# Slot tables and one-hot blocks of a two-layer mixture-of-experts kernel: from fp32r to bf16 in parts

## Chip, cores and metric

The kernel runs on one core of a Trainium2 chip. The metric is the time of one execution on the device in microseconds (us); of several executions the median is taken. Three runs of the kernel before gave 2065.88, 2066.47 and 2069.43 us.

## What is computed

Two transformer layers over 512 tokens of width 1024. Each has a dense part (attention and a second mixer, with their projections) and then a layer of experts. For the experts a router picks, for each token, 2 of 32 experts in the first layer and 8 of 64 in the second, each with a weight; every expert is a gated feed-forward network with 256 hidden columns, and a token's result is the weighted sum over its experts.

```python
# first layer                                  # second layer
g_w, g_idx = lax.top_k(g_prob, 1)              e_w: top 8 of sigmoid(router) + bias,
e_w, e_idx = lax.top_k(softmax(e_sel), 2)      normalised, times 2.5
weights = g_w * e_w / sum(e_w)
ys = ragged_dot(silu(ragged_dot(xs, w_gate, sizes)) * ragged_dot(xs, w_up, sizes), w_down, sizes)
out = einsum('nkd,nk->nd', ys, weights)
```

All weights are f32. Those of the experts are 3 MB each, so 96 MB in the first layer and 192 MB in the second, and every expert is read once.

## The kernel before

The kernel is one long program in which a planner lays out the instructions of all engines. Work is written as tasks (Python generators); `Flow` wakes the task that is due, and a clock of its own (`Clock.note`) reckons what each instruction will take on its engine. Nearly every instruction goes through the wrapper at line 131, so all rows of the profile bear L131 and are told apart by their tiles. The order that comes out is fixed: each engine works off its own queue in it.

**Layout of the program.** Dense part of the first layer, then its expert loop (`Experts.run`, some 400 to 690 us), a dense part of the second layer, its expert loop (some 1380 to 2040 us), and the last norm. While a dense part still runs, SP already loads the first experts' weights into free buffers. The weights are loaded in chunks of 512 KB, six an expert (four for gate and up, two for down), into tiles named `w` and `wx`; SP issues the load for a chunk when a buffer is given back. Experts are visited in an order made from their counts, and each place in it has a planned number of slots (`PLAN1`, `PLAN2`: blocks of 16 to 128 slots).

**Routing.** `Route.tile` finds for each of the four tiles of 128 tokens which experts are chosen (`sel`) and with which weight. `Route.finish` (from line 2000) puts them in the order of the experts by matmuls with a permutation, writes that order to `self.order` (SP reads it for the addresses of the weights), counts slots by matmuls with a triangle and with ones in bf16 (`slots`, `counts`), and fills the table `R`: for each expert and each of the four token tiles, 128 rows of four fp32r numbers, which are the slot number (0 where the expert is not chosen), the token number + 1, and the weight in a rounded part and the rest. The token numbers are put there early by `Route.table` (line 1903) on GpSimd. The split of the weight is ACT (rounded copy), then DVE (the rest); DVE then writes the slot numbers.

**A block of slots.** `Experts.block` (line 2224) turns a part of the table into the list of tokens of one block: DVE compares the slot numbers with a row of numbers (`ios`, bf16) and gives a one-hot block `oh` (128 tokens x C slots, for four token tiles); PE multiplies it by `R` in four matmuls into four columns; DVE makes the index (`iv`, out of range where the slot is empty) and the weight from these in four small operations; GpSimd gathers the rows of the tokens (`xg`) with an indirect DMA. Blocks are made up to three ahead of their use (`AHEAD`). The first three are made in `begin` (their one-hot blocks are `h` tiles). In `run` the first loads into the extra buffers `wx` wait for the first gather (`b.gate`).

**An expert.** PE transposes the gathered rows (`xT`), multiplies by gate and up, ACT and DVE make the activation (`a`, times the weight), PE transposes it (`aT`) and multiplies by down, ACT and DVE bring the result out (`y`), and GpSimd adds it to the sum in memory with an indirect DMA (`acc_d`). `Experts.rest` (line 2447) is a loop for experts that hold more tokens than planned; the number of its turns is known at run time.

Of the kernel before, what the change touches and what calls it, by code (L numbers as in the profile page):

```python
# [10 lines left out]
F32 = mybir.dt.float32  # L11
F32R = mybir.dt.float32r
BF16 = mybir.dt.bfloat16
I32 = mybir.dt.int32
U32 = mybir.dt.uint32
AF = mybir.ActivationFunctionType
ALU = mybir.AluOpType
AX = mybir.AxisListType
# [3 lines left out]
P = 128  # L22
# [3 lines left out]
NT = T // P  # L26
# [1836 lines left out]
class Route:  # L1863
# [38 lines left out]

    def table(self, pool):
        b, nc = self.b, self.b.nc
        self.R = pool.tile([P, self.E, NT, 4], F32R, name="R")
        tok = b.small(NT)
        nc.gpsimd.iota(tok, pattern=[[P, NT]], base=1, channel_multiplier=1, allow_small_or_imprecise_dtypes=True)
        nc.gpsimd.tensor_copy(self.R[:, :, :, 1], tok.unsqueeze(1).to_broadcast([P, self.E, NT]))

    def tile(self, t, h, keep=None):  # L1910

# [88 lines left out]
    def finish(self):  # L2000

        b, nc, E, F = self.b, self.b.nc, self.E, self.first
        while len(self.sels) < NT or not self.chosen:
            yield 1
        yield W
        rank = yield from self.ranks(NT, True)
        oh = b.h()[:E, :E]
        nc.vector.tensor_scalar(out=oh, in0=self.rank[:E], scalar1=rank, scalar2=None, op0=ALU.is_equal)
        while None in self.parts:
            yield 1  # L2010
        yield W
        po, ps = yield from b.banks(2)
        nc.tensor.matmul(po[:, 0:E], self.iop[:E].to_broadcast([E, P]), oh, start=True, stop=True)
        ps = ps[:, : NT * 2 * E].rearrange("p (t c e) -> p t c e", t=NT, c=2)
        for c in range(2):
            for t in range(NT):
                nc.tensor.matmul(ps[:, t, c], self.parts[t][:, c], oh, start=True, stop=True)
        yield W
        sels = b.h(BF16)[:, : NT * E].rearrange("p (t e) -> p t e", t=NT)
        nc.vector.tensor_copy(sels, ps[:, :, 0])  # L2020
        nc.vector.tensor_copy(self.order[:, F:], po[:, F:E])
        self.known(E)
        yield W
        for t in range(NT):
            self.slots(po[:, (t + 1) * E : (t + 2) * E], [sels[:, u] for u in range(NT)], t)
        et = lambda c: self.R[:, :, :, c].rearrange("p e t -> p t e")
        b.split(ps[:, :, 1], et(2), et(3))
        yield W
        nc.vector.scalar_tensor_tensor(out=et(0), in0=po[:, E : (NT + 1) * E].rearrange("p (t e) -> p t e", t=NT), scalar=1.0, in1=sels, op0=ALU.add, op1=ALU.mult)
        self.counts(po[:, (NT + 1) * E : (NT + 2) * E], [sels[:, t] for t in range(NT)])  # L2030
        nc.scalar.activation(self.orow, po[:, 0:E], AF.Copy)
        yield W
        nc.scalar.activation(self.cnt, po[:, (NT + 1) * E : (NT + 2) * E], AF.Copy)
        b.back(2)
# [45 lines left out]
class Router1:  # L2080


    n = 36
# [50 lines left out]
class Router2:  # L2134


    n = 64
# [25 lines left out]
class Experts:  # L2163
# [57 lines left out]
        for g in self.xgs:  # L2221
            self.b.nc.gpsimd.memset(g, 0.0)

    def block(self, R, n, C, oh):


        b, nc = self.b, self.b.nc
        x = SimpleNamespace(n=self.n, C=C, xg=self.xgs.popleft() if self.xgs else self.ring[self.n % 4])
        self.n += 1
        oh = oh("oh", F32R)[:, : NT * C].rearrange("p (t c) -> p t c", t=NT)  # L2230
        nc.vector.tensor_tensor(out=oh, in0=b.ios[:, n : n + C].unsqueeze(1).to_broadcast([P, NT, C]),
                                in1=R[:, :, 0].bitcast(F32).unsqueeze(2).to_broadcast([P, NT, C]), op=ALU.is_equal)
        yield
        pt, = yield from b.banks(1)
        for t in range(NT):
            nc.tensor.matmul(pt[:C, 0:4], oh[:, t], R[:, t], start=(t == 0), stop=(t == NT - 1))
        yield
        v = b.const.tile([P, 4], F32, name="iv", tag="iv", bufs=8)[:C]
        it = v[:, 2:3].bitcast(I32)
        nc.vector.scalar_tensor_tensor(out=v[:, 1:2], in0=pt[:C, 1:2], scalar=0.0, in1=b.beyond[:C], op0=ALU.is_equal, op1=ALU.mult)  # L2240
        nc.vector.scalar_tensor_tensor(out=it, in0=pt[:C, 1:2], scalar=-1.0, in1=v[:, 1:2], op0=ALU.add, op1=ALU.add)
        nc.vector.tensor_copy(v[:, 1:2], pt[:C, 3:4])
        nc.vector.tensor_tensor(out=v[:, 0:1], in0=pt[:C, 2:3], in1=v[:, 1:2], op=ALU.add)
        b.back(1)
        x.idx, x.w = it, v[:, 0:1]
        x.dma = nc.gpsimd.indirect_dma_start(out=x.xg[:C], out_offset=None, in_=self.h2_d, in_offset=bass.IndirectOffsetOnAxis(ap=it, axis=0),
                                             bounds_check=T - 1, oob_is_err=False)
        return x
# [126 lines left out]

    def fetched(self, i, n, C):
        r = self.route
        self.xs[i].append((yield from self.block(r.R[:, i], sum(r.plan[i][:n]), C, self.oh)))

    def run(self, nx, after={}):  # L2380
        b, nc, E, r = self.b, self.b.nc, self.E, self.route
# [65 lines left out]
    def rest(self, K):  # L2447

        b, nc, E = self.b, self.b.nc, self.E
# [5 lines left out]
        wx = lambda name, dt=F32: x_.pool.tile([P, 1024], dt, name=name, tag=x_.tag, bufs=x_.cap)  # L2455
        n = nc.values_load(ovr[0:1, 3:4], min_val=0, max_val=E + T * K // P)  # L2456
        with b.tc.If(n > 0):
            with b.tc.For_i(0, n, 1) as i:
                ev, place = (nc.values_load(ovr[0:1, bass.ds(i * 4 + k, 1)], min_val=0, max_val=E - 1) for k in (0, 2))
                R, sv = self.mp.tile([P, NT, 4], F32R, name="rR"), self.mp.tile([P, 1], F32, name="rs")  # L2460
                nc.sync.dma_start(R.bitcast(F32), self.route.R.bitcast(F32)[:, bass.ds(place, 1)].rearrange("p o t c -> p (o t) c"))
                nc.sync.dma_start(sv, self.route.lsv[bass.ds(i, 1)].rearrange("o p -> p o"))
                nc.vector.tensor_scalar(out=R[:, :, 0], in0=R[:, :, 0].bitcast(F32), scalar1=sv, scalar2=None, op0=ALU.subtract)
                gu, dn = self.weights(ev)
                ws = []

                def load():
                    if len(ws) < 6:
                        ws.append(wx("w"))
                        nc.sync.dma_start(ws[-1], self.part(gu, dn, len(ws) - 1))  # L2470

                load()
                load()
                self.n = 0
                x = b.at_once(self.block(R, 0, P, wx))
                self.xT(x)

                for c in range(4):
                    self.gu(x, c, ws[c])
                    load()  # L2480
                self.act(x)
                self.aT(x)
                for c in range(2):
                    self.dn(x, c, ws[4 + c])
                    load()
                self.add(x)
# [117 lines left out]
```

## Time and profile before

| | |
|---|---|
| median of three runs | 2066.47 us (2065.88 to 2069.43) |
| the profiled execution | 2071.1 us, of which the span of the profile is 2069.3 us |
| mean granted clock of TensorE | 0.932 |
| PE busy (matmuls) | 1805.0 us, 87% |
| DVE busy | 1098.4 us, 53% |
| ACT busy | 641.6 us, 31% |
| GpSimd (POOL) busy | 321.4 us, 16% |
| moved by DMA | 549.72 MB, mean 266 GB/s |

PE is TensorE's matmuls, PEld its weight loads, DVE VectorE, ACT ScalarE, POOL GpSimd and SP the queue that issues most DMAs (the letter q behind an engine means its queue). A row of a timeline gives start and length in us, engine, line, operation, tiles out<-in, shape and count; in brackets stands the idle time of the engine before it and what ended that. A row of waits gives who waited for whom, the total in us, how often, and the longest. The shares of the whole span mix stages with different limits, so the rows further on are of single stretches.

### The profile page before, as it was taken

How to read it: one execution, taken by the hardware profiler on the slowest of the kernel's cores; microseconds unless marked ns; L12 is line 12 of the kernel's file. 1: busy time of each engine (PE TensorE's matmuls, PEld its weight loads, DVE VectorE, ACT ScalarE, POOL GpSimd, SP SyncE). 2: the span in 40 equal slices, each digit the busy share in tenths (PEclk: the TensorE clock that was granted, in tenths of full speed). 3: DMA queues.
4: the chain of work that ended last, by engine and by line, in shares of the span. 5: the costliest groups of instructions: out<-in, count | busy, mean ns of one | idle time of the engine just before them, and what ended most of it. 6: DMA issues, size and time to landing. Idle time of an engine off the chain costs nothing. (4 is left out here: it accounts for less than half of the span.)

```text
span 2069.3 us, 36349 instructions
## 1 busy us (share of the span) xinstructions
PE 1805.0 (87%) x13053; PEld 1162.7 (56%) x13053; DVE 1098.4 (53%) x3182; ACT 641.6 (31%) x1443; POOL 321.4 (16%) x359
## 2 busy tenths in 40 slices
PE   4999978498877579889999998889999999999993
PEld 3777764354344467667767677664544445455551
DVE  5554763543333365456655565765554455555553
ACT  3522452222222242356653223421211112211121
POOL 1000000123222000000000311022322222222221
PEclk9999988599976699999999999999999999999997
DMA  9745424499999956775423556569999999999996
GB/s 340 270 161 195 154 79 186 159 352 371 376 382 382 335 182 210 262 216 160 147 85 112 183 181 247 192 210 359 361 369 352 356 357 359 360 353 348 345 356 222
DMA packets 179019, 549.72 MB, mean 266 GB/s; under 512 B 27650, under 2 KB 40066, under 8 KB 178836
## 3 DMA queue, kind: packets, MB, share of 16 engines
q1 hardware_dynamic: 158116, 488.98, 64.7%
q0 software_dynamic: 18560, 54.88, 10.7%
q10 hardware_dynamic: 2160, 3.50, 0.5%
q8 instruction: 105, 1.72, 0.3%
q14 instruction: 78, 0.64, 0.1%
HBM read 493.38 MB, written 60.51 MB: 268 GB/s over the span
## 5 line engine op out<-in xcount | busy, mean ns | idle before, releaser
L131 PE MATMUL bank<-w,xT 128*32 128x128 f32 (+5 forms) x2988 | 309.5, 359 | 13.5 <-DMA w<-in_w_gu 12.0
L131 PE MATMUL bank<-u,hi 128*128 128x512 f32 x800 | 263.0, 411 | 10.6 <-DVE u L131 5.6
L131 ACT ACTIVATE xT<-bank,k,k 128x32 f32<-128x32 f32 (+6 forms) x412 | 132.9, 406 | 448.8 <-PE bank L131 395.8
L131 POOL DMA_INDIRECT acc_d<-y,iv x103 | 149.4, 1451 | 495.8 <-DVE y L131 163.3
L131 PEld LDWEIGHTS bank<-w,xT 128*32 128x32 f32 (+5 forms) x2988 | 147.5, 126 | 130.2 <-issue 68.6
L131 PE MATMUL bank<-wx,xT 128*32 128x128 f32 (+4 forms) x1812 | 188.3, 369 | 12.7 <-ACT xT L131 6.0
L131 DVE TENSOR_TENSOR y<-bank,gate 32x256 f32<-32x256 f32 (+5 forms) x228 | 128.0, 561 | 108.3 <-PE bank L131 106.1
L131 PEld LDWEIGHTS bank<-u,hi 128*128 128x128 f32 x800 | 148.8, 196 | 45.6 <-DVE u L131 7.0
L131 PE MATMUL bank<-u,lo 128*128 128x512 f32 x400 | 161.9, 405 | 11.3 <-DVE lo L131 11.2
L131 PE MATMUL bank<-hi,u 128*128 128x512 f32 (+1 forms) x512 | 152.7, 383 | 0.0
L131 DVE TENSOR_TENSOR lo<-w,hi 128x1024 fp32r<-128x1024 f32 x97 | 126.3, 1307 | 38.3 <-ACT hi L131 37.5
L131 PEld LDWEIGHTS bank<-ident,xg 48*128 48x128 f32 (+6 forms) x824 | 99.0, 199 | 73.8 <-issue 71.4
L131 PE MATMUL bank<-w,aT 128*32 128x256 f32 (+5 forms) x664 | 124.8, 525 | 12.5 <-DMA w<-in_w_dn 8.8
L131 PEld LDWEIGHTS bank<-wx,xT 128*32 128x32 f32 (+4 forms) x1812 | 91.9, 131 | 77.7 <-issue 40.5
L131 PE MATMUL bank<-wx,aT 128*32 128x256 f32 (+5 forms) x600 | 119.0, 524 | 8.7 <-DMA wx<-in_w_dn 8.5
L131 DVE TENSOR_SCALAR xT<-bank,k,k 128x32 f32<-128x32 f32 (+6 forms) x412 | 113.3, 339 | 18.5 <-PE bank L131 15.4
L131 PE MATMUL bank<-ident,xg 48*128 48x48 f32 (+6 forms) x824 | 112.1, 279 | 9.9 <-DMA xg<-ha_d,iv 9.5
L131 PE MATMUL bank<-lo,u 128*128 128x512 f32 (+1 forms) x256 | 103.7, 405 | 9.7 <-DVE lo L131 9.0
L131 ACT ACTIVATE hi<-w 128x1024 fp32r<-128x1024 f32 x97 | 100.7, 1049 | 35.7 <-PE bank L131 16.9
L131 PEld LDWEIGHTS bank<-hi,u 128*128 128x128 f32 x512 | 96.0, 192 | 16.8
L131 POOL DMA_INDIRECT xg<-hb_d,iv x71 | 71.0, 1000 | 163.3 <-PE bank L131 69.1
L131 PEld LDWEIGHTS bank<-u,lo 128*128 128x128 f32 x400 | 78.0, 195 | 32.0 <-DVE lo L131 14.7
(234 smaller groups left out, 2503.2 us busy)
## 6 DMA issues: line engine op xcount, KB each, us to landing
w<-in_w_gu SPq DMA_DIRECT2D x235, 512.0 KB
wx<-in_w_gu SPq DMA_DIRECT2D x149, 512.0 KB
w<-in_w_dn SPq DMA_DIRECT2D x101, 512.0 KB
wa<-in_w_ada SPq DMA_DIRECT2D x96, 512.0 KB
wx<-in_w_dn SPq DMA_DIRECT2D x91, 512.0 KB
w<-in_w_in SPq DMA_DIRECT2D x68, 512.0 KB
w<-in_w_out SPq DMA_DIRECT2D x21, 512.0 KB
nab<-in_nab SPq DMA_DIRECT2D x48, 128.0 KB
```

Of the source, the lines that this page charges most:

```text
L131: r = f(*a, **k)
```

## The change

- The slot numbers move to a table of their own, `S`, in f32. `R` becomes bf16 with six numbers a row: the token number in two parts (the place within the tile + 1, and 128 times the tile), both whole numbers that bf16 holds, the weight in three parts, each the bf16 rounding of what the ones before leave, and a zero that is not multiplied.
- `table` on GpSimd makes two index fills and two copies in place of one of each, and sets the sixth number to zero.
- `finish` makes the three parts: ACT rounds, DVE subtracts, ACT rounds the rest, and DVE subtracts again, before it writes the slot numbers. It uses one more `h` tile.
- `block` makes the one-hot block in bf16, from slots in f32, and multiplies it by five bf16 columns. The index comes from the sum of the first two columns, the weight from the sum of the other three: two of the four small operations become reductions, and the index is the third of the four where it was the second.
- `rest` loads `S` and `R` apart, one DMA more a turn.

```diff
     def table(self, pool):
-        self.R = pool.tile([P, self.E, NT, 4], F32R, name="R")
-        tok = b.small(NT)
-        nc.gpsimd.iota(tok, pattern=[[P, NT]], base=1, channel_multiplier=1, allow_small_or_imprecise_dtypes=True)
-        nc.gpsimd.tensor_copy(self.R[:, :, :, 1], tok.unsqueeze(1).to_broadcast([P, self.E, NT]))
+        self.S, self.R = pool.tile([P, self.E, NT], F32, name="S"), pool.tile([P, self.E, NT, 6], BF16, name="R")
+        for c, step, base, m in ((0, 0, 1, 1), (1, P, 0, 0)):
+            tok = b.small(NT)
+            nc.gpsimd.iota(tok, pattern=[[step, NT]], base=base, channel_multiplier=m, allow_small_or_imprecise_dtypes=True)
+            nc.gpsimd.tensor_copy(self.R[:, :, :, c], tok.unsqueeze(1).to_broadcast([P, self.E, NT]))
+        nc.gpsimd.memset(self.R[:, :, :, 5], 0.0)
...
     def finish(self):
-        b.split(ps[:, :, 1], et(2), et(3))
+        r = b.h()[:, : NT * E].rearrange("p (t e) -> p t e", t=NT)
+        nc.scalar.activation(et(2), ps[:, :, 1], AF.Copy)
+        nc.vector.tensor_tensor(out=r, in0=ps[:, :, 1], in1=et(2), op=ALU.subtract)
+        nc.scalar.activation(et(3), r, AF.Copy)
         yield W
-        nc.vector.scalar_tensor_tensor(out=et(0), in0=po[:, E : (NT + 1) * E].rearrange("p (t e) -> p t e", t=NT), scalar=1.0, in1=sels, op0=ALU.add, op1=ALU.mult)
+        nc.vector.tensor_tensor(out=et(4), in0=r, in1=et(3), op=ALU.subtract)
+        nc.vector.scalar_tensor_tensor(out=self.S.rearrange("p e t -> p t e"), in0=po[:, E : (NT + 1) * E].rearrange("p (t e) -> p t e", t=NT), scalar=1.0, in1=sels, op0=ALU.add, op1=ALU.mult)
...
-    def block(self, R, n, C, oh):
+    def block(self, S, R, n, C, oh):
-        oh = oh("oh", F32R)[:, : NT * C].rearrange("p (t c) -> p t c", t=NT)
+        oh = oh("oh", BF16)[:, : NT * C].rearrange("p (t c) -> p t c", t=NT)
         nc.vector.tensor_tensor(out=oh, in0=b.ios[:, n : n + C].unsqueeze(1).to_broadcast([P, NT, C]),
-                                in1=R[:, :, 0].bitcast(F32).unsqueeze(2).to_broadcast([P, NT, C]), op=ALU.is_equal)
+                                in1=S.unsqueeze(2).to_broadcast([P, NT, C]), op=ALU.is_equal)
...
-            nc.tensor.matmul(pt[:C, 0:4], oh[:, t], R[:, t], start=(t == 0), stop=(t == NT - 1))
+            nc.tensor.matmul(pt[:C, 0:5], oh[:, t], R[:, t, 0:5], start=(t == 0), stop=(t == NT - 1))
...
-        nc.vector.scalar_tensor_tensor(out=v[:, 1:2], in0=pt[:C, 1:2], scalar=0.0, in1=b.beyond[:C], op0=ALU.is_equal, op1=ALU.mult)
-        nc.vector.scalar_tensor_tensor(out=it, in0=pt[:C, 1:2], scalar=-1.0, in1=v[:, 1:2], op0=ALU.add, op1=ALU.add)
-        nc.vector.tensor_copy(v[:, 1:2], pt[:C, 3:4])
-        nc.vector.tensor_tensor(out=v[:, 0:1], in0=pt[:C, 2:3], in1=v[:, 1:2], op=ALU.add)
+        nc.vector.scalar_tensor_tensor(out=v[:, 1:2], in0=pt[:C, 0:1], scalar=0.0, in1=b.beyond[:C], op0=ALU.is_equal, op1=ALU.mult)
+        nc.vector.tensor_reduce(out=v[:, 3:4], in_=pt[:C, 0:2], op=ALU.add, axis=AX.X)
+        nc.vector.scalar_tensor_tensor(out=it, in0=v[:, 3:4], scalar=-1.0, in1=v[:, 1:2], op0=ALU.add, op1=ALU.add)
+        nc.vector.tensor_reduce(out=v[:, 0:1], in_=pt[:C, 2:5], op=ALU.add, axis=AX.X)
...
     def rest(self, K):
-                R, sv = self.mp.tile([P, NT, 4], F32R, name="rR"), self.mp.tile([P, 1], F32, name="rs")
-                nc.sync.dma_start(R.bitcast(F32), self.route.R.bitcast(F32)[:, bass.ds(place, 1)].rearrange("p o t c -> p (o t) c"))
+                S, R, sv = self.mp.tile([P, NT], F32, name="rS"), self.mp.tile([P, NT, 6], BF16, name="rR"), self.mp.tile([P, 1], F32, name="rs")
+                nc.sync.dma_start(S, self.route.S[:, bass.ds(place, 1)].rearrange("p o t -> p (o t)"))
+                nc.sync.dma_start(R, self.route.R[:, bass.ds(place, 1)].rearrange("p o t c -> p (o t) c"))
```

## Rows read from the trace of the kernel before

**Rows 1.** Busy time by stretch: window, its length, engines, granted clock, DMA share, GB/s.

```profile
core 0: us, PE busy (x) PEld busy (x) DVE busy (x) ACT busy (x) POOL busy (x), PEclk, DMA share, GB/s
420.00:686.00 266.00, 224.18 (x2100) 118.92 (x2102) 99.62 (x395) 67.19 (x193) 68.27 (x58) 0.85 1.03 374
560.00:580.00 20.00, 15.34 (x135) 7.71 (x134) 6.70 (x26) 4.37 (x12) 4.63 (x4) 1.00 1.03 377
600.00:620.00 20.00, 15.49 (x211) 9.77 (x209) 7.33 (x34) 5.41 (x17) 4.58 (x4) 0.65 1.03 383
1400.00:2036.00 636.00, 620.18 (x5126) 313.62 (x5122) 336.47 (x1078) 120.45 (x366) 167.59 (x134) 1.00 1.03 356
```

**Rows 2.** Waits of SP's queue from 1400 to 2036 us.

```profile
SPq L131 <- DMA w<-in_w_gu: 153.9, 128, 3.5
...
SPq L131 <- DMA wx<-in_w_gu: 67.7, 60, 2.9
SPq L131 <- PE bank L131: 23.1, 80, 0.9
```

**Rows 3.** Waits of PE: first from 420 to 686, then from 1400 to 2030 us.

```profile
PE bank L131 <- DMA w<-in_w_gu: 12.0, 16, 1.6
...
PE bank L131 <- DMA w<-in_w_gu: 0.6, 1, 0.6
PE bank L131 <- DMA wx<-in_w_gu: 0.5, 1, 0.5
```

**Rows 4.** Timeline of PE and its weight loads, end of the second loop.

```profile
2034.12 0.17 PEld L131 LDWEIGHTS bank<-w,aT 128*48 128x48 f32 x4 [1.01 <-DMA w<-in_w_dn]
...
2039.26 0.81 PE L131 MATMUL bank<-w,aT 128*32 128x256 f32 x8 [0.96 <-SPq L2457]
2040.94 1.08 PE L131 MATMUL bank<-w,aT 128*32 128x256 f32 x8 [0.87 <-SPq L2457]
```

**Rows 5.** Busy time by stretch of the instructions on `oh` alone: PE, PEld, DVE.

```profile
1400.00:2036.00 636.00, 29.45 (x260) 22.52 (x260) 29.22 (x65) 1.00 1.03 356
...
420.00:686.00 266.00, 8.86 (x108) 6.55 (x108) 8.63 (x27) 0.85 1.03 374
```

**Rows 6.** Timeline: one group on the table, what follows it, ten bf16 matmuls.

```profile
1701.13 0.70 PE L131 MATMUL bank<-R,oh 128*48 128x4 f32 x4
...
1701.69 4.68 PE L131 MATMUL bank<-w,aT 128*128 128x512 f32 x12
...
1348.80 0.47 PE L131 MATMUL bank<-h,c 128*128 128x64 bf16 x10
```

**Rows 7.** Timeline of finish() and the first blocks, first layer.

```profile
392.68 0.39 ACT L131 ACTIVATE R<-bank 128x128 fp32r<-128x128 f32 x1 [7.53 <-DVE h L131]
...
393.10 0.37 DVE L131 TENSOR_TENSOR R<-bank,R 128x128 fp32r<-128x128 f32 x1 [0.36 <-ACT R L131]
393.38 0.36 DVE L131 SCALAR_TENSOR_TENSOR R<-bank,h 128x128 fp32r<-128x128 f32 x1
...
393.77 1.10 DVE L131 TENSOR_TENSOR h<-ios,R 128x256 fp32r<-128x256 bf16 x3
...
394.94 0.15 DVE L131 SCALAR_TENSOR_TENSOR iv<-bank,beyond 64x1 f32<-64x1 f32 x1
...
396.12 1.03 POOL L131 DMA_INDIRECT xg<-ha_d,iv  x1 [15.81 <-DVE iv L131]
...
405.25 1.11 PE L131 MATMUL bank<-ident,xg 64*128 64x64 f32 x8 [9.50 <-DMA xg<-ha_d,iv]
```

**Rows 8.** Timeline of finish() and the first blocks, second layer.

```profile
1350.16 0.58 DVE L131 SCALAR_TENSOR_TENSOR R<-bank,h 128x256 fp32r<-128x256 f32 x1
...
1350.79 0.28 PE L131 MATMUL bank<-h,c 128*128 128x64 bf16 x4 [0.74 <-DVE R L131]
...
1352.36 0.81 PE L131 MATMUL bank<-R,h 128*64 128x4 f32 x12
```

**Rows 9.** Timeline of POOL: its first work after the second layer's table.

```profile
1296.99 0.62 POOL L131 DMA_DIRECT2D hb_d<-u  x1 [35.99 <-DVE u L131]
```

**Rows 10.** Timeline of DVE: a reduction over 64 columns.

```profile
1395.45 0.21 DVE L131 TENSOR_REDUCE s<-h 128x1 f32<-128x64 f32 x1
```

More of the change, by code (lines that the diff above doesn't have):

```diff
@@ L2377, in fetched @@
         r = self.route
-        self.xs[i].append((yield from self.block(r.R[:, i], sum(r.plan[i][:n]), C, self.oh)))
+        self.xs[i].append((yield from self.block(r.S[:, i], r.R[:, i], sum(r.plan[i][:n]), C, self.oh)))
     def run(self, nx, after={}):
@@ L2459, in rest @@
                 ev, place = (nc.values_load(ovr[0:1, bass.ds(i * 4 + k, 1)], min_val=0, max_val=E - 1) for k in (0, 2))
-                R, sv = self.mp.tile([P, NT, 4], F32R, name="rR"), self.mp.tile([P, 1], F32, name="rs")
-                nc.sync.dma_start(R.bitcast(F32), self.route.R.bitcast(F32)[:, bass.ds(place, 1)].rearrange("p o t c -> p (o t) c"))
+                S, R, sv = self.mp.tile([P, NT], F32, name="rS"), self.mp.tile([P, NT, 6], BF16, name="rR"), self.mp.tile([P, 1], F32, name="rs")
+                nc.sync.dma_start(S, self.route.S[:, bass.ds(place, 1)].rearrange("p o t -> p (o t)"))
+                nc.sync.dma_start(R, self.route.R[:, bass.ds(place, 1)].rearrange("p o t c -> p (o t) c"))
                 nc.sync.dma_start(sv, self.route.lsv[bass.ds(i, 1)].rearrange("o p -> p o"))
-                nc.vector.tensor_scalar(out=R[:, :, 0], in0=R[:, :, 0].bitcast(F32), scalar1=sv, scalar2=None, op0=ALU.subtract)
+                nc.vector.tensor_scalar(out=S, in0=S, scalar1=sv, scalar2=None, op0=ALU.subtract)
                 gu, dn = self.weights(ev)
@@ L2474, in rest @@
                 self.n = 0
-                x = b.at_once(self.block(R, 0, P, wx))
+                x = b.at_once(self.block(S, R, 0, P, wx))
                 self.xT(x)
```

## The prediction

> **What bounds the kernel now.** I read the busy time by stretch first, then who the two queues that matter (SP, which issues the weight loads, and PE) waited for, and last the end of the second expert loop. The stretches show two loops in which everything the change touches runs: the first loop, 266 us, and the second, 636 us [rows 1]. In both the 16 DMA engines count as busy all the time (share 1.03), at 374 and 356 GB/s. PE is busy 224.18 of 266 us in the first loop, but 620.18 of 636 us in the second. So in the first loop the weights are the bound: PE stands waiting for them there, 12.0 us for the largest of four kinds of chunk [rows 3]. In the second loop both look full, and the two views of waits must decide. SP, before it issued a load, waited 359.8 us in all (four kinds, 295 times) for an earlier load of its own to land, and 23.1 us (80 times) for PE to give back a buffer [rows 2]. PE until 2030 us waited for weights twice, 1.1 us in all [rows 3]. That means: the loads run at their own pace and not at PE's, and PE lives on chunks that landed earlier. At the very end this store is used up. PE stands 1.01 us before the second down half of expert 62, 0.96 and 0.87 us before the two of expert 63 [rows 4]; the last two waits carry the name of the branch behind the loop, but each stands before the first matmul of a fresh chunk, so I read them as landings too. The end of the second loop is therefore set by the stream of weights, with PE a fraction of a microsecond behind it.
>
> **The change, part by part.** *Small matmuls.* Each block of slots multiplies its one-hot block by the table in four matmuls; their operands go from fp32r to bf16 (four columns become five). In the second loop 65 blocks cost 29.45 us of busy PE, 0.45 us a block; in the first 27 cost 8.86 us, 0.33 us a block [rows 5]. One group seen alone: it starts at 1701.13 and the next matmul at 1701.69, so it holds PE 0.56 us. The bf16 matmuls of the trace that come nearest, the counting ones in finish(), take 0.47 us for ten, so 0.19 us for four [rows 6]; four with a handoff took 0.28 us [rows 8]. Saved per block: 0.45 - 0.19 = 0.26 at most by the means, 0.45 - 0.28 = 0.17 at least; I take 0.2. That is 65 x 0.2 = 13 us of PE work in the second loop, and 27 x 0.14 = 4 us in the first (0.33 - 0.19). I cost it at nothing: in both loops the weights arrive no sooner for it. If that cover were gone the 13 us would be a gain (first rival).
>
> What the row says of the cover: 374 GB/s in the first loop against 356 in the second at the same busy share [rows 1]. [...] At the first loop's rate the second loop's bytes would fit into 636 x 356/374 = 605 us, and all 13 us could come out, so the rival stays.
>
> *One-hot blocks on DVE.* One operand, the slots, stays f32, the output gets narrower. 65 of them take 29.22 us [rows 5], and DVE has 300 us free in that stretch [rows 1]. Whether they stay as they are or lose half, nothing waits for it: 0.
>
> *The index and the weight of a block.* Four DVE operations of 0.15 us [rows 7] stay four, two of them now sums over 2 and 3 columns; the nearest reduction, over 64 columns, took 0.21 us [rows 10]. So between 0 and 0.12 us more a block, off the path except for the first gather. The index is now the third of the four and not the second: 0.18 us later if the gather waits for it alone, nothing if it waits for all four.
>
> *The three parts of the weight, in finish().* Before: ACT 0.39, DVE 0.37, DVE 0.36 (slots), then the first blocks [rows 7]. After, ACT rounds the rest once more and DVE subtracts once more before the slots. The second rounding costs between 0.36 (the DVE pass over the same 128 columns) and 0.39 us (its twin on ACT); I take 0.37. The subtraction costs 0.37 as its twin. That is +0.74 us, plus 0.03 us for each of the two handoffs, so +0.8. The faster matmuls give nothing back here: DVE makes the three one-hot blocks from 393.77 to 394.87 and the first index operation comes at 394.94, so at most 0.07. With the index the first gather starts at 396.12 + 0.7 to 1.0 us. PE waited 9.50 us for it, until 405.25 [rows 7], and SP's next loads (those behind the gate in run()) wait for the same landing. The weights that were issued before are in flight in that time, so the delay reaches the stream between not at all and in full: 0 to 1.0, I take half of 0.8, +0.4.
>
> In the second layer finish() runs under the shared expert's matmuls. PE already stands 0.74 us for the slots before four counting matmuls, because they share a PSUM bank [rows 8]; the new subtraction stands ahead of the slots on DVE (0.58 us for the slots at this width, so 0.4 to 0.6 us), and what is queued behind it on DVE are the one-hot blocks and then the dense layer's own work. PE gets back part of it at once: twelve matmuls in 0.81 us [rows 8] become some 0.57. Net +0.2 to +0.4 on PE, and the weight stream starts later, behind stores that wait for loads, so -0.2 to +0.4; I take +0.1.
>
> *Tables.* GpSimd gets one more index fill, one more copy and a fill of zeros. After the table of the second layer it had nothing to do for 35.99 us [rows 9]: 0. In the first layer the table is made at the start and first read at 393 us [rows 7]: 0. finish() takes one more buffer of the h ring, so tiles behind it take over a buffer one place younger; I cost that at 0, within the 1.5 us of the order below.
>
> *The overflow loop* (rest()) gets one more load per turn, but no turn of it is in the trace. No other DMA is added or moved.
>
> *Order.* The instructions are laid out by the planner's clock, and the diff changes what it reckons (two of the four small operations become cheaper by 0.064 us, finish() gets two more). An order that comes out otherwise around the second finish() can shift the start of the stream; the wait of 0.74 us there is the size of one such step, so I allow two of them either way, 1.5 us.
>
> **Sum.** Against the profiled execution: 2071.1 + 0 (PE) + 0.4 + 0.1 = 2071.6 us. The median of the three runs is 2066.47, 4.6 below it, so the forecast is 2066.5 + 0.5 = 2067.0 us.
>
> **The rivals.** *PE is the bound of the second loop (faster).* For it: 620.18 of 636 us busy, and only 1.1 us of waiting for weights until 2030. Then a shorter PE frees buffers sooner, loads go out sooner, and the 13 us come out: 2067.0 - 13 = 2054. Against it: SP waited 15 times as long for its own loads as for PE, and PE's waits at the end. It decides at the end of the loop: if PE still had unread chunks there it would be the bound. A part of it, up to the 23.1 us that SP did wait for PE, is possible.
>
> [...]
>
> *The change does not do what it says:* bf16 weights of 16 to 128 columns load no faster and the groups keep 0.45 us. Then the time is the same 2067.
>
> **How the numbers follow.** Forecast 0.74, PE bound 0.14, clock 0.10, no effect 0.02. Bounds of the terms: first layer 0 to +1.0, second -0.2 to +0.4, order -1.5 to +1.5, and the runs themselves reached 0.6 below and 3.0 above their median. Below: 2066.5 - 0.2 - 1.5 - 0.6 = 2064.2; above: 2066.5 + 1.0 + 0.4 + 1.5 + 2 = 2071.4, not all of the 3.0 since a median is compared. Toward the first rival the range goes on to 2061.5 (5.5 of the 13 us), and it ends above at 2071.5. A difference under 0.2% (4.1 us) can't be told from none. The forecast lies within it but for 0.03 on either side; with the rivals: faster 0.17, same 0.70, slower 0.13.
>
> **What would show it.** Right: the groups on the table take about half of their 0.45 us, PE's busy time in the second loop falls by some 13 us, PE's waits for weights in its second half rise by about as much, and DMA share and GB/s stay; the first gather starts some 0.8 us later. Wrong: the second loop ends earlier by several us with PE still without waits (PE was the bound), or the clock of the second loop shows stretches under 1.00 near its end.

## The result and the profile after

The changed kernel takes 2083.60 us (median of four runs, 2078.47 to 2084.99), the kernel before 2066.18 us beside it (four runs, 2064.94 to 2069.43). The ratio is 1.0060 with a 95% interval of 1.0035 to 1.0085: slower, by 7 to 18 us. The profiled execution of the changed kernel is its fastest, 2078.47 us with a span of 2076.7 us; that of before took 2071.1 us, so the two traces show 7.4 us of the difference.

The two expert loops are not where it went. Busy time by stretch after the change, with columns as in [rows 1]; under it the same view for the instructions on `oh` alone, as in [rows 5] (PE, PEld, DVE, clock, DMA share, GB/s):

```profile
420.00:686.00 266.00, 214.51 (x2082) 116.02 (x2078) 93.70 (x391) 65.22 (x188) 67.64 (x58) 0.87 1.03 373
...
1400.00:2036.00 636.00, 614.12 (x5112) 308.18 (x5112) 330.07 (x1102) 121.72 (x370) 166.75 (x135) 1.00 1.03 357
...
420.00:686.00 266.00, 6.79 (x108) 6.83 (x108) 8.64 (x27) 0.87 1.03 373
1400.00:2036.00 636.00, 18.32 (x264) 14.24 (x264) 29.77 (x66) 1.00 1.03 357
```

The groups on the table fell from 29.45 to 18.32 us of PE in the second loop. DMA share and GB/s stayed. PE's busy time in that window fell by 6.1 us. SP still waits for its own loads and hardly for PE, as in [rows 2] (view of waits, SP from 1400 to 2036 us: us in all, times, longest):

```profile
SPq L131 <- DMA w<-in_w_gu: 156.3, 126, 3.5
...
SPq L131 <- PE bank L131: 20.7, 73, 0.6
```

The loss lies ahead of the second loop, at two kinds of place. The first is finish(). Timeline of ACT, DVE, PE and POOL in the second layer after the change, to be held against [rows 8]:

```profile
1353.83 1.38 ACT L131 ACTIVATE R<-bank 128x256 bf16<-128x256 f32 x1 [5.01 <-DVE h L131]
...
1355.24 0.61 DVE L131 TENSOR_TENSOR h<-bank,R 128x256 f32<-128x256 f32 x1 [1.32 <-ACT R L131]
...
1355.88 1.38 ACT L131 ACTIVATE R<-h 128x256 bf16<-128x256 f32 x1 [0.68 <-DVE h L131]
1357.29 1.33 DVE L131 TENSOR_TENSOR R<-h,R 128x256 bf16<-128x256 f32 x1 [0.31 <-ACT R L131]
1358.23 0.84 DVE L131 SCALAR_TENSOR_TENSOR S<-bank,h 128x256 f32<-128x256 f32 x1
...
1359.12 0.37 PE L131 MATMUL bank<-h,c 128*128 128x64 bf16 x4 [3.13 <-DVE S L131]
...
1363.75 1.03 POOL L131 DMA_INDIRECT xg<-hb_d,iv  x1 [17.13 <-DVE iv L131]
```

Every operation that writes bf16 into the table takes 1.33 to 1.38 us. The one rounding of before (fp32r) took 0.61 us, in its timeline:

```profile
1347.88 0.61 ACT L131 ACTIVATE R<-bank 128x256 fp32r<-128x256 f32 x1 [5.25 <-DVE h L131]
```

PE stands 3.13 us for the slots where it stood 0.74. Behind this idle time the granted clock of this trace falls to 0.50. Windows of the trace after, ahead of the idle time, in it and behind it:

```profile
1340.00:1356.00 16.00, 14.41 (x92) 10.96 (x92) 8.16 (x34) 3.93 (x9) 2.79 (x3) 1.00 0.37 138
1356.00:1359.00 3.00, 0.00 (x0) 0.00 (x0) 2.69 (x3) 1.26 (x1) 0.00 (x0) 0.98 0.00 0
1359.20:1362.20 3.00, 3.00 (x11) 1.96 (x11) 1.00 (x3) 1.62 (x3) 0.00 (x0) 0.50 0.00 0
```

By the source the neighbours in such a write lie 48 bytes apart, for the other three token tiles stand between them (64 bytes before); taken together the entries of one part stand at every 12th byte, hence "steps of 12 bytes" below.

The first layer shows the same writes at half the width (timeline after, against [rows 7]):

```profile
391.11 0.76 ACT L131 ACTIVATE R<-bank 128x128 bf16<-128x128 f32 x1 [7.52 <-DVE h L131]
...
392.30 0.79 ACT L131 ACTIVATE R<-h 128x128 bf16<-128x128 f32 x1 [0.44 <-DVE h L131]
...
393.12 0.74 DVE L131 TENSOR_TENSOR R<-h,R 128x128 bf16<-128x128 f32 x1 [0.85 <-ACT R L131]
393.48 0.62 DVE L131 SCALAR_TENSOR_TENSOR S<-bank,h 128x128 f32<-128x128 f32 x1
...
404.24 1.11 PE L131 MATMUL bank<-ident,xg 64*128 64x64 f32 x8 [8.58 <-DMA xg<-ha_d,iv]
```

The second place has nothing of the change in it: the dense part of the second layer from 880 to 900 us, where all engines have the order of instructions that they had before. DVE waits longer there for a load of `in_nab`. Timeline of DVE, first before, then after:

```profile
892.59 0.43 DVE L131 CUSTOM_DVE_ANT_0 bank<-bank,nab 128x256 f32<-128x256 f32 x1 [4.20 <-DMA nab<-in_nab]
```

```profile
896.06 0.43 DVE L131 CUSTOM_DVE_ANT_0 bank<-bank,nab 128x256 f32<-128x256 f32 x1 [7.69 <-DMA nab<-in_nab]
```

What else the DMA engines did in the 4 us behind the load `nav<-vk_d` that goes ahead of it in SP's queue (the page's DMA section, that window: packets, MB, share of 16 engines), first before (881.24 to 885.24 us), then after (881.48 to 885.48):

```profile
q1 hardware_dynamic: 1233, 0.86, 72.2%
```

```profile
q1 hardware_dynamic: 1167, 0.82, 64.8%
q8 instruction: 1, 0.02, 3.8%
```

In the changed kernel a 16 KB piece of code (queue q8 instruction: 105 packets, 1.72 MB in the whole trace) is fetched among the loads. Before, it came at 880.6 us, ahead of them. Each load has 16 landing events in the trace, read here as one from each of the 16 engines; DVE's operation on in_nab starts 0.13 us behind the last of them before (landing at 892.46 us) and 0.14 us after (895.92). Fifteen of the events come within 1.1 us, before and after; after the change the last one comes up to 3.02 us behind the fifteenth, for thirteen loads in a row, while before the greatest such lag there was 0.22 us. The piece itself took 2.44 us there and 0.96 before; in the other nine traces with a late engine it took 1.02 to 2.10 us. That its own time is a part of the lag is an estimate from these figures, and what makes up the rest is not shown.

### The profile page after: what moved, and what is told of

Same layout as the page of the kernel before. It is cut to its first block, busy times and chain, and to the rows that moved or that the text cites. A ratio compares the mean times of both kernels' runs of the same rounds, so it can differ in the third digit from the quotient of the medians.

```text
span 2076.7 us, 36323 instructions
## 1 busy us (share of the span) xinstructions
PE 1786.0 (86%) x13053; PEld 1151.5 (55%) x13053; DVE 1084.3 (52%) x3184; ACT 645.0 (31%) x1445; POOL 323.8 (16%) x365
## 3 DMA queue, kind: packets, MB, share of 16 engines
q8 instruction: 105, 1.72, 0.3%
## 5 line engine op out<-in xcount | busy, mean ns | idle before, releaser
L131 PE MATMUL bank<-ident,xg 48*128 48x48 f32 (+6 forms) x824 | 112.0, 279 | 13.1 <-DMA xg<-ha_d,iv 8.6
```

The lines of the kernel that those rows point to most:

```text
L131: r = f(*a, **k)
```

## The experiments

Names with a_ start from the changed kernel, those with b_ from the kernel before. Each ratio is to the kernel before, run beside it on the same chip, with its 95% interval; 0.001 is 2.1 us.

**a_again.** No edit.

> The changed kernel once more, for a second trace of it. Theory A (finish() of the second layer): the chain ACT, DVE, ACT, DVE, DVE from the counts' copy to the slots is 4.4 us longer than before and PE stands 3.1 us for the slots at about 1359 us again, with a stretch of low clock behind it; that costs 3.4 us in every execution. Theory B (the dense part of the second layer, where the order of instructions is that of before): the 3.5 us later landing of a load of in_nab at 892 us comes again. Rival C: that landing is the chance of one execution, and the second trace loses its time at another place. Time 2078 to 2085 by all of them.

Ratio 1.0045 (1.0026 to 1.0063). The chain in finish() has the same lengths (ACT 1.38 and 1.38, DVE 1.33 us, PE idle for 3.13), and the load of in_nab lands late again (13.6 us behind the issue of nav, 14.4 in the first trace, 11.2 before). So both come from the program and not from one execution. Behind the idle time the granted clock is 0.50 once more; in a_2, the same kernel a third time, PE stands 3.11 us there and the clock stays at 1.00. Windows behind the idle time, a_again and then a_2:

```profile
1357.00:1363.00 6.00, 6.00 (x25) 4.46 (x25) 1.16 (x13) 0.89 (x1) 2.71 (x3) 0.50 0.13 37
```

```profile
1355.60:1361.60 6.00, 6.00 (x39) 4.79 (x39) 2.56 (x16) 2.51 (x5) 2.25 (x3) 1.00 0.08 23
```

**a_slots_first.** The slots ahead of the weight's parts:

```
         et = lambda c: self.R[:, :, :, c].rearrange("p e t -> p t e")
+        nc.vector.scalar_tensor_tensor(out=self.S.rearrange(...), ...)
...
         nc.vector.tensor_tensor(out=et(4), in0=r, in1=et(3), op=ALU.subtract)
-        nc.vector.scalar_tensor_tensor(out=self.S.rearrange(...), ...)
```

> As changed, but in finish() the slots are written to S ahead of the parts of the weight, so that PE's counting matmuls need no part of the weight. Theory A: PE's idle time before the four counting matmuls falls from 3.13 us to under 1 us, no low clock behind it, and the kernel ends some 3 us sooner than the changed one (2083.6 to about 2080.5). Theory B (loss in the dense part before it): no difference in the end, 2083.6, for the order of everything up to 1345 us is the same.

Ratio 1.0026 (1.0009 to 1.0043), the median 2.7 us under a_again's. PE's idle time at the four counting matmuls is gone; a short one stands at the blocks instead. Timeline of PE in this kernel:

```profile
1359.74 0.29 PE L131 MATMUL bank<-h,c 128*128 128x64 bf16 x4
...
1362.05 0.94 PE L131 MATMUL bank<-R,h 128*64 128x5 bf16 x12 [0.54 <-DVE h L131]
```

The first gather starts 7.9 us after the chain's first copy, 10.4, 9.5 and 9.0 in the three traces of the change, 6.5 before. That fits theory A, but the two intervals overlap, so the gain is not shown by the times alone. Some of the loss is left.

**a_flat.** The table part by part, so that a part of all experts lies in one run:

```
-pool.tile([P, self.E, NT, 6], BF16, name="R")
+pool.tile([P, 6, NT, self.E], BF16, name="R")
...
-        et = lambda c: self.R[:, :, :, c].rearrange("p e t -> p t e")
+        et = lambda c: self.R[:, c]
...
-            nc.tensor.matmul(pt[:C, 0:5], oh[:, t], R[:, t, 0:5], ...)
+            nc.tensor.matmul(pt[:C, 0:5], oh[:, t], R[:, 0:5, t], ...)
```

> As changed, but the table of tokens and weights lies part by part ([128, 6, 4, experts]), so that finish() writes each part in one run of 512 bytes and not to elements 12 bytes apart. Theory A1 (scattered writes of two bytes are slow): ACT's two roundings take 0.6 and not 1.38 us, DVE's last part 0.5 and not 1.33 us, PE's idle time at the counting matmuls falls from 3.13 to about 1 us, and the kernel ends 2 to 3 us sooner than the changed one. Rival A2 (rounding to bf16 is slow however it is written): 1.38 and 1.33 us as before, and no gain. The moving operand of a block's matmuls then has its five columns 512 bytes apart; the groups stay at about 0.2 us if that costs nothing.

Ratio 1.0023 (1.0005 to 1.0041), the median 6.6 us under a_again's, more than the 2 to 3 expected. The order of instructions is that of the change. Timeline of finish(), second layer:

```profile
1347.79 0.38 ACT L131 ACTIVATE R<-bank 128x256 bf16<-128x256 f32 x1 [5.07 <-DVE h L131]
...
1348.66 0.42 ACT L131 ACTIVATE R<-h 128x256 bf16<-128x256 f32 x1 [0.49 <-DVE h L131]
...
1349.68 0.42 DVE L131 TENSOR_TENSOR R<-h,R 128x256 bf16<-128x256 f32 x1
...
1350.67 0.28 PE L131 MATMUL bank<-h,c 128*128 128x64 bf16 x4 [0.71 <-DVE S L131]
...
1353.90 1.03 POOL L131 DMA_INDIRECT xg<-hb_d,iv  x1 [13.34 <-DVE iv L131]
```

The writes are 3.2 to 3.6 times as fast, PE's idle time is that of before (0.71 against 0.74), and the extra rounding and the extra subtraction cost next to nothing any more in this layer (first gather at 6.58 us from the first copy, 6.48 before). A1 holds, A2 falls. Moving operands 512 bytes apart cost next to nothing: the groups take 18.44 us in the second loop, 18.32 in the change. But 4.8 us over the kernel before (1.0 to 8.5) are left, and the late engine is in this trace too.

**b_one_more_h.** In the kernel before, finish() gets one more line, `b.h()`.

> The kernel before, but finish() takes one buffer more of the h ring and does nothing with it, as the change does: a shift of buffers by one place, by which the planner lays out both expert loops in another order, with no operation added. Theories A and B (the operations of finish() and of the tables cost the time): 2066 as before, within 2 us. Rival D (an order of the loops that came out otherwise, whatever the cause, costs the time): 5 us or more above the kernel before.

Ratio 0.9996 (0.9975 to 1.0017). The expected other order did not come: in the two traces every engine has the same instructions in the same order through both loops. So this run shows that the shift of buffers costs nothing, and leaves rival D open. The square below settles it: a_flat with its code ahead of the load has the changed kernel's order on every engine and the time of before.

**a_flat_24 and b_104.** Tiny matmuls with no other use, ahead of the first transposes of the first loop:

```
             pt = b.bank().rearrange("p (j q) -> p j q", j=4)
+            for _ in range(self.pad):
+                b.nc.nc.tensor.matmul(pt[:32, 0, 0:1], b.ios[:, 0:32], b.ios[:, 0:1], start=True, stop=True)
+            self.pad = 0
...
+        self.pad = 24 if E == 32 else 0
         turn(0)
```

> a_flat with 24 tiny bf16 matmuls more (48 PE instructions) ahead of the first transposes of the first expert loop, where PE stands 9 us for the gather: PE's program behind them lies 48 instructions further on, nothing else differs. Theory F (code fetch): PE's code comes in 16 KB pieces over the same DMA engines; in the kernel before one piece comes at 880.6 us, 0.6 us ahead of the load nav<-vk_d, in the four traces of the changed kernels at 882.6 to 885.0, behind it, and one of the 16 engines then lands 1.5 to 3 us after the others for all loads of 885 to 896. Moved by 48 instructions the piece comes some 3 us earlier relative to the load: no late engine, the stretch from the first operation on in_nab of the second layer to the fourteenth takes 54 to 56 us (59.2 in a_flat), and the kernel ends some 3 to 4 us sooner than a_flat. Rival C (chance): 58 to 60 us or any other value, time as a_flat.

> The kernel before with 104 tiny bf16 matmuls more (208 PE instructions, 48 short of one 16 KB piece of code) at the same place, so that the pieces behind come some 3 us later relative to the work. Theory F: the piece of 880.6 us comes at about 883.5, behind the load nav<-vk_d, one engine lands late, the stretch of the fourteen operations on in_nab takes 58 to 60 us (53.9 before), and the kernel ends 3 to 4 us later than before, unless other pieces gain. Rival C: 54 to 56 us, time as before. The matmuls themselves are some 5 us of PE in a wait of 9.5 us and cost nothing by either.

a_flat_24: ratio 0.9994 (0.9979 to 1.0010). b_104: 1.0024 (1.0010 to 1.0038), 5 us over the kernel before, with nothing of the change in it. The pieces moved as expected: in a_flat_24 to 2.3 us ahead of the load, with no late engine, in b_104 to 3.3 us behind it, with one 2.7 us late. DVE's row for the load of in_nab in a_flat_24 reads as before:

```profile
892.18 0.43 DVE L131 CUSTOM_DVE_ANT_0 bank<-bank,nab 128x256 f32<-128x256 f32 x1 [4.13 <-DMA nab<-in_nab]
```

**a_flat_twice.** The matmuls on the table twice in the second layer: `for t in list(range(NT)) * (2 if self.E == 64 else 1)`.

> a_flat, but each block of the second expert loop does its matmuls on the table twice: PE gets back the 13 us that the change saves there. Theory of the prediction (the weights bound the loop): no difference from a_flat (within 2 us), PE busy some 10 to 13 us more between 1400 and 2036 us. Rival G (a shorter PE harms: more idle PE, lower clock, or another rhythm of the loads): faster than a_flat by several us. Rival P (PE is the bound): up to 13 us slower.

Ratio 1.0030 (1.0013 to 1.0048) against 1.0023 for a_flat, each to the kernel before on its own chip. The groups take 27.02 us of PE in the second loop in place of 18.44, so 8.6 us are given back where 10 to 13 were expected (windows on `R`):

```profile
1400.00:2036.00 636.00, 27.02 (x528) 0.00 (x0) 0.00 (x0) 0.00 (x0) 1.00 1.03 356
```

From the first transposes of the second loop to PE's last matmul it takes 667.4 us, a_flat 667.9. In between PE falls up to 9.7 us behind a_flat (at about 1805 us) and is level again at the end: it has chunks in store, and the weights set the end. Rival G falls by the time, and a PE that bounds the whole loop falls by the two traces. By the ratios alone less than some 5 us either way is not resolved.

**b_steps.** Behind the kernel before, three writes of each kind on ACT and DVE (one execution, read by its trace alone):

```
+        for n, dt, w in (("f4", F32, 1), ("f16", F32, 4), ("b2", BF16, 1), ("b4", BF16, 2), ("b12", BF16, 6), ("b16", BF16, 8)):
+            for r in range(3):
...
+                nc.scalar.activation(a[:, :, 0], src, AF.Copy)
+                nc.vector.tensor_copy(v[:, :, 0], src)
+                nc.vector.tensor_tensor(out=x[:, :, 0], in0=src, in1=src, op=ALU.subtract)
```

> The kernel before, and behind it ACT and DVE write 128x256 results of a small test three times each: f32 one behind the other, f32 at steps of 16 bytes, bf16 one behind the other, and bf16 at steps of 4, 12 and 16 bytes. Theory A1: bf16 one behind the other is as fast as f32 or faster (0.3 to 0.4 us), bf16 at steps of 4 bytes or more costs over twice as much (some 1.3 us), f32 at 16 bytes about 0.6 us at most. Rival A2 (only steps matter): f32 at 16 bytes as slow as bf16 at 12. Up to the test it is the kernel before: the stretch of the fourteen operations on in_nab takes 54 to 56 us by theory F.

Costliest groups of this test (busy us, mean ns of one); the number in a name is the step in bytes, b is bf16, f is f32, A is ACT, X a DVE subtraction, V a DVE copy. The two engines ran side by side:

```profile
L1818 DVE TENSOR_TENSOR b16X<-src 128x256 bf16<-128x256 f32 x3 | 4.6, 1528 | 0.0
L1816 ACT ACTIVATE b16A<-src 128x256 bf16<-128x256 f32 x3 | 4.1, 1378 | 0.0
L1818 DVE TENSOR_TENSOR b12X<-src 128x256 bf16<-128x256 f32 x3 | 3.2, 1077 | 0.0
L1816 ACT ACTIVATE b12A<-src 128x256 bf16<-128x256 f32 x3 | 3.1, 1045 | 0.1
...
L1816 ACT ACTIVATE f16A<-src 128x256 f32<-128x256 f32 x3 | 2.0, 661 | 0.1
...
L1818 DVE TENSOR_TENSOR f16X<-src 128x256 f32<-128x256 f32 x3 | 1.8, 615 | 0.0
L1816 ACT ACTIVATE b4A<-src 128x256 bf16<-128x256 f32 x3 | 1.5, 488 | 0.1
...
L1818 DVE TENSOR_TENSOR b4X<-src 128x256 bf16<-128x256 f32 x3 | 1.3, 441 | 0.0
L1818 DVE TENSOR_TENSOR b2X<-src 128x256 bf16<-128x256 f32 x3 | 1.3, 419 | 0.0
...
L1816 ACT ACTIVATE b2A<-src 128x256 bf16<-128x256 f32 x3 | 1.2, 416 | 0.1
L1816 ACT ACTIVATE f4A<-src 128x256 f32<-128x256 f32 x3 | 1.2, 411 | 12.3 <-DVE b2X L1818 12.3
```

The rival called A2 here (only the step counts) falls: at 16 bytes f32 takes 661 ns and bf16 1378, and bf16 at 12 bytes 1045. A1 was half right: bf16 at 4 bytes costs 488 ns, hardly more than in one run (416), so it is the wide step and the two-byte element together.

**The square of both causes.** a_24, a_152: the changed kernel with 24 and with 152 tiny matmuls. a_flat_128, a_flat_152: a_flat with 128 and 152. a_2, a_flat_2, a_flat_3, a_flat_24_2: kernels above once more.

> The changed kernel with the 24 tiny matmuls of a_flat_24, its table written to steps of 12 bytes as the change does. It completes the square of two causes (steps of the table, place of the code piece). If both are real and add up: the piece comes 2 to 3 us ahead of the load nav<-vk_d, no engine lands over 0.3 us late there, the chain in finish() of the second layer stays at 9.5 to 10.4 us from its first copy to the first gather, and the time lies 3 to 5 us over the kernel before (ratio about 1.002), 4 to 6 us under the change. Rival S (steps alone cost it): ratio 1.0045 as the change. Rival F alone (place of the code alone): ratio 1.000.

> a_flat with 128 tiny matmuls: 256 PE instructions, just one 16 KB piece of code, so that the pieces behind fall at the same places of the work as in a_flat. Theory F: the piece comes some 3 us behind nav<-vk_d as in a_flat, one engine lands 2.6 to 3.0 us late, ratio to before 1.002 as a_flat. Rival H (what helped in a_flat_24 was the busy PE ahead of the loop, not the place of the code): no loss, ratio 0.9994 or less.

> a_flat once more, beside the other three on one chip. Theory F: piece behind nav<-vk_d, an engine 2.6 to 3.0 us late, ratio 1.002. If the place of the code costs nothing in the end (rival C): the same ratio as a_flat_24_2.

> a_flat_24 once more, on the same chip as a_flat_2 and a_flat_128. Theory F: piece ahead of nav<-vk_d, no late engine there, 4 to 6 us under a_flat_2 and a_flat_128, ratio to before 0.999 to 1.000. Rival C: the same ratio as a_flat_2.

> The changed kernel, as the corner of a square on one chip: table at steps of 12 bytes or in one run, code piece behind or ahead of nav<-vk_d. From the runs so far (differences of means to the kernel before): steps cost 5 to 7 us, the piece behind the load 1.5 to 3.5 us. So 8 to 9 us over before, ratio 1.004.

> The changed kernel with 152 tiny matmuls ahead of the first expert loop (one whole 16 KB piece and 48 instructions, the place of a_24 by other means). If place of the code counts: piece ahead of nav<-vk_d, no engine over 0.3 us late there, 1.5 to 3.5 us under a_2. Rival C: as a_2.

> a_flat, third corner: piece behind the load, one engine 2 to 3 us late, 5 to 7 us under a_2, 3 to 4 us over before.

> a_flat with 152 tiny matmuls, fourth corner: piece ahead of the load, no late engine there; if the place counts in the end, 1.5 to 3.5 us under a_flat_3 and within 1.5 us of before. Rival C: as a_flat_3.

Ratios: a_24 1.0033 (1.0018 to 1.0047), a_152 1.0036 (1.0020 to 1.0052), a_2 1.0050 (1.0031 to 1.0069); a_flat_2 1.0018 (1.0003 to 1.0032), a_flat_3 1.0024 (1.0009 to 1.0038), a_flat_128 1.0009 (0.9994 to 1.0023); a_flat_24_2 1.0010 (0.9991 to 1.0030), a_flat_152 0.9998 (0.9982 to 1.0014). a_24 came out higher than expected, a_flat_128 lower. a_flat_152 lies 5.4 us under a_flat_3 where 1.5 to 3.5 were expected, a_flat_24_2 only 1.7 under a_flat_2 where 4 to 6 were, and alone it would not have shown the effect of the place. The means of each corner (without the first four runs of the change, 1.0060):

```
                     piece behind the load       piece ahead of it            behind - ahead
steps of 12 bytes    1.0048 (a_again, a_2)       1.0035 (a_24, a_152)         0.0013
one run              1.0019 (a_flat, _2, _3,     1.0001 (a_flat_24, _24_2,    0.0018
                             _128)                       _152)
steps - run          0.0029                      0.0034
```

The steps cost 0.0029 and 0.0034, 6 to 7 us; the place of the code costs 0.0013 and 0.0018, about 3 us; within the noise the two add up. What is left of the change without both is 0.0001. With intervals of some 0.0016 either side on one ratio, each side of the square is uncertain by 0.0013 to 0.0017, so the 3 us are sure in sign only by all four corners together; b_104, with 0.0024 from the place alone, agrees. a_flat_128, whose pieces fall as in a_flat, has the late engine as a_flat has. Its time lies between those of a_flat and a_flat_24, so it does not exclude rival H (a busier PE ahead of the loop helps); b_104, with a busier PE and a later end, speaks against H.

The eighteen traces side by side. "First copy" is DVE's copy of the choices (`h<-bank`), which starts 0.33 us (first layer) and 0.46 us (second) ahead of ACT's first write into the table. Columns: when the piece comes, counted from the issue of nav<-vk_d; the greatest lag of the sixteenth engine in the loads behind it; landing of the next in_nab load, from the same issue; the stretch from the first operation on in_nab of the second layer to the fourteenth. Then, from the chain's first copy in finish() of the first layer to the first gather, and to the first matmul of the next dense part (bank<-hc,hi); from there to the first copy in the second layer's finish(); from that to its first gather; and to PE's last matmul. All in us, worked out from the traces:

```
               piece   lag  lands stretch |  gather  loop 1   dense  gather  loop 2
before         -0.66  0.22  11.2   53.9 |  3.77  310.1  645.0   6.48  694.6
b_one_more_h   -0.69  0.14  10.8   56.3 |  3.78  309.5  643.1   6.49  692.0
b_steps        -0.85  0.03  11.1   56.7 |  3.77  311.2  643.2   6.50  692.4
b_104           3.28  2.71  13.7   60.4 |  3.77  310.5  645.9   6.50  693.6
after           1.08  3.02  14.4   60.2 |  5.59  312.4  650.2  10.38  695.0
a_again         2.82  2.56  13.6   58.5 |  5.59  312.6  645.2   9.50  698.9
a_2             2.47  3.06  13.9   58.3 |  5.59  310.0  647.1   8.98  695.3
a_24           -0.64  0.19  10.9   56.0 |  5.60  310.2  646.0  10.36  696.2
a_152          -1.92  0.09  11.1   56.9 |  5.60  311.0  645.6   8.99  696.9
a_slots_first   1.04  3.00  14.1   59.2 |  5.17  311.1  652.0   7.92  690.6
a_flat          2.88  2.79  13.6   59.2 |  4.18  309.9  643.2   6.58  693.9
a_flat_2        2.67  1.85  13.5   59.4 |  4.17  310.7  645.5   6.56  693.7
a_flat_3        0.83  2.21  13.1   57.5 |  4.17  309.6  642.4   6.55  694.3
a_flat_128      3.19  2.63  13.6   60.4 |  4.18  309.9  646.2   6.56  695.6
a_flat_twice    3.18  2.88  13.8   59.2 |  4.18  310.5  646.3   6.70  693.7
a_flat_24      -2.32  0.14  11.0   56.4 |  4.17  310.7  642.1   6.56  692.3
a_flat_24_2    -1.45  0.19  11.0   56.7 |  4.18  310.1  643.0   6.55  693.7
a_flat_152     -1.53  0.45  11.4   55.9 |  4.17  310.2  642.2   6.57  692.4
```

In all ten with the piece behind the load an engine is 1.85 to 3.06 us late and the in_nab load lands 13.1 to 14.4 us after the issue; in all eight with the piece ahead the lag is at most 0.45 and the load lands at 10.8 to 11.4. The stretch takes 57.5 to 60.4 us against 53.9 to 56.9: 59.2 against 56.1 in the mean. The column "dense" says the same for each table by itself: behind the load it is longer by 2.2 us (fp32r table), 1.7 (steps) and 2.3 (one run) in the mean.

## Why the prediction was wrong

It said 2067.0 us and no measurable change; it was slower by 7 to 18 us. By its steps:

*Small matmuls at nothing: right.* They took 18.32 in place of 29.45 us in the second loop and 6.79 in place of 8.86 in the first, 11 and 2 us where 13 and 4 were reckoned. Nothing of it reached the end: the loads ran at 357 GB/s as before, and a_flat_twice, which gives 8.6 us of it back, does not end measurably later. So the bound was read rightly, and *PE is the bound* was rightly put low. Two signs that were named for it did not come: PE's busy time between 1400 and 2036 us fell by 6.1 us and not by 13, and PE's waits for weights until 2030 us rose only from 1.1 to 2.1 us. More of the free time went into waits for gathered rows (0.2 us before, 4.4 after) and for DVE's `a` (11.6, 14.3).

*One-hot blocks, the four small operations: right. The tables: nearly.* 29.77 us for 66 blocks against 29.22 for 65 [rows 5]; the reductions take 0.14 us, less than the 0.21 of [rows 10]. POOL's table fills take 1.85 + 1.53 + 1.18 us where they took 1.44, and POOL stands idle for 33.14 us behind them. But they were not free for DVE. Timeline of POOL and DVE, first after, then a_flat:

```profile
1266.00 1.53 POOL L131 CAST R<-s 128x256 bf16<-128x256 f32 x1
1266.54 2.94 DVE L131 TENSOR_TENSOR lo<-w,hi 128x1024 fp32r<-128x1024 f32 x2
1267.21 1.18 POOL L131 MEMSET R<- 128x256 bf16 x1
```

```profile
1261.66 0.31 POOL L131 MEMSET R<- 128x256 bf16 x1
1262.18 2.53 DVE L131 TENSOR_TENSOR lo<-w,hi 128x1024 fp32r<-128x1024 f32 x2
```

In all six traces with steps the first of these two subtractions runs beside POOL's fills and takes 1.61 to 1.62 us; in the eight with one run the fills are over before it, and it takes 1.21.

*The three parts of the weight: the term that failed.* The step priced each new operation "as its twin", 0.37 us, by rows of fp32r writes [rows 7]. The order of the chain was right, and that PE waits for slots which now stand behind the subtraction. But a bf16 write into this table is no twin of an fp32r write: 0.76, 0.79 and 0.74 us in the first layer, 1.38, 1.38 and 1.33 in the second. First layer: the gather starts 5.59 us behind the first copy in place of 3.77, so +1.8 where +0.7 to +1.0 stood. To the end of the loop it is 311.2 us in the mean of the five traces with steps of 12 bytes and the change's order of slots, against 310.3 in the four of before. That would be about half, as taken, but the single traces overlap. Second layer: PE's idle time grew by 2.4 us where +0.2 to +0.4 stood, and the gather starts 2.5 us later, up to 3.9 where the clock fell too. From the first copy to PE's last matmul those five traces take 696.5 us in the mean, the four of before 693.2. About 1 us more lies between POOL's fills and that copy (88.8 us against 87.9), of which DVE's 0.4 us beside the fills is a part. That makes 0.9 + 3.3 + 1.0 = 5.2 of the 6 to 7 us that the runs give to the steps, from one trace a run; the rest is not assigned.

The step alone does not set the price: in b_steps bf16 at 4 bytes took 488 ns against 416 in one run, and at 16 bytes f32 took 661 and bf16 1378 ns. The size of the element counts too.

*What the prediction had no term for: the place of the code.* It said of the dense part only that the order could shift by 1.5 us. The order there did not shift at all; a piece of code did. In the four traces of the changed kernel and its twin in slots (after, a_again, a_2, a_slots_first) it comes 1.7 to 3.5 us later against the loads than before, and that costs about 3 us. Why the change moves it (its program for PE is longer by a little ahead of that point, or lies otherwise) was not tried.

A piece holds some 256 of PE's instructions: from 1054.7 to 1239.8 us of the trace before seven pieces pass, with 890 matmuls, 890 weight loads and 11 semaphore instructions of PE, 255.9 a piece, and with the 256 instructions of a_flat_128 the piece comes 3.19 us behind the load, in a_flat 2.88. In all ten traces in which it comes among the loads one engine is late, by 1.85 to 3.06 us; in the eight in which it comes ahead of them the lag is at most 0.45 us.

*The clock: it fell, but in other places, and its cost is not resolved.* The 0.10 for the clock stood for a stretch of low clock near the end of the second loop and 7 us lost by it. No run shows that loss; in the trace after the granted clock is 1.00 from 2000 to 2020 and from 2020 to 2040 us. It fell behind the idle time that the prediction itself had named, the one before the four counting matmuls, in three of the five traces (after, a_again, a_24); in a_2 and a_152 PE stood as long and the clock stayed at 1.00. With the fall the gather comes 9.5 to 10.4 us behind the first copy, without it 9.0; to PE's last matmul it is 696.7 and 696.1 us in the mean. The clock also fell while PE waited for the late load. Windows from 892 to 902 us, first before (1.00), then after (0.66):

```profile
892.00:902.00 10.00, 7.96 (x70) 6.16 (x71) 5.63 (x16) 4.61 (x9) 0.00 (x0) 1.00 0.42 108
```

```profile
892.00:902.00 10.00, 4.72 (x16) 3.73 (x15) 2.42 (x9) 2.01 (x3) 0.00 (x0) 0.66 0.48 137
```

That fall is not the late engine's alone. Counting from the issue of nav<-vk_d, the clock falls to 0.50 at 12.5 to 14.7 us in 16 of the 18 traces: in all ten with a late engine (for 6.8 us in eight, 3.4 in two) and in six of the eight without one (for 3.4 us).

*Order of the loops: right.* The changed kernel has another order in both loops. a_flat_24, a_flat_24_2 and a_flat_152 have that same order, and in the mean the time of before (1.0001).

## What to carry to other kernels

Price a write by its element size and its step, not by an operation of the same width beside it: here 256 bf16 results a partition took ACT 416 ns in one run and 1045 at steps of 12 bytes, 256 f32 results 411 in one run and 661 at 16 bytes (b_steps), and one run for each column of the table was worth 6 to 7 us. When a program's code moves, loads far from the edit can land later (here 13.1 to 14.4 us behind the issue of nav in place of 10.8 to 11.4); so measure a small edit also with its code shifted by a fraction of a 16 KB piece (here by 24 tiny matmuls) before its few us are put down to the edit itself. And an operation that is off every busy engine's path can still stand ahead of the one that PE waits for (here 3.13 us of idle PE in place of 0.74).

## What the hardware showed

- Writes of 256 two-byte results a partition (b_steps): 416 ns in one run, 488 at 4 bytes, 1045 at 12, 1378 at 16 on ACT; 419, 441, 1077 and 1528 for a DVE subtraction. Four-byte results at 16 bytes: 661 and 615.
- With a 16 KB piece of code among the loads the last of a load's 16 landings came up to 1.85 to 3.06 us behind the fifteenth (ten traces of ten), for 8 to 13 loads over 1 us behind it; with the piece ahead of them the greatest lag was 0.45 us (eight of eight).
- A DVE subtraction of 1024 columns took 1.61 to 1.62 us beside GpSimd's fills at steps of 12 bytes, 1.21 where the fills were over.
- Behind 3.11 to 3.13 us of an idle PE the granted clock fell to 0.50 in three traces and stayed at 1.00 in two; behind 0.71 and 0.74 us of idle it stayed at 1.00.
